# A hybrid encoder trunk in split fp32 on one core: the borders between its stages rebuilt

## The chip, the core and the metric

The kernel runs on one core of a Trainium2 chip. TensorE (PE) multiplies; its clock has two levels, 2.4 GHz and 1.2 GHz, and a profile gives the level as a share of the full one. VectorE (DVE), ScalarE (ACT) and GpSimd (POOL) do the element work, and SyncE (SP) issues nearly all DMAs, in one order. Each engine takes its instructions strictly in the order in which they stand in its own queue. The metric is the device time of one launch in microseconds, the median of three runs.

## The reference

Two layers (DEPTH = 2) over 640 tokens: 512 of one prompt, and 8 sequences of 16. A layer has three stages; each takes the residual `x`, norms and modulates it, and adds its own normed, gated output:

```
for l in range(DEPTH):
    h = rmsnorm(x, norm_g[l,0]) * (1 + sc1) + sh1
    x = x + 0.5 * g1 * rmsnorm(swiglu(h, w_ffn1[l,0], w_ffn3[l,0], w_ffn2[l,0]), norm_g[l,1])
    h = rmsnorm(x, norm_g[l,2]) * (1 + sc2) + sh2
    y, states = token_mixer(h, ...)      # 1024 -> 5640 columns, attention, mLSTM, w_pa, w_pb, w_out
    x = x + g2 * rmsnorm(y, norm_g[l,3])
    h = rmsnorm(x, norm_g[l,4]) * (1 + sc3) + sh3
    x = x + 0.5 * g3 * rmsnorm(swiglu(h, w_ffn1[l,1], w_ffn3[l,1], w_ffn2[l,1]), norm_g[l,5])
```

D_MODEL is 1024, D_FF 2816. `sh`, `sc`, `g` come from `silu(c) @ w_ada + b_ada`, one row for the prompt and one for each of the 8 sequences. All of it is fp32.

## The kernel before

**Numbers.** Each large fp32 product is three products of fp32r parts: an operand is split into `hi` (ACT copies it to fp32r) and `lo = x - hi` (DVE, sometimes POOL subtracts), and `three` issues hi·hi, hi·lo, lo·hi. So every weight slab and every activation costs an ACT cast and a subtraction before PE may use it.

**Tiles.** The 640 tokens are five tiles of 128 rows (tile 4 is the 8 sequences), and in the transposed layout, where a tile of `h` holds 128 channels by 640 tokens, two halves of 320 tokens, t=0 and t=1. Tiles 0 and 1 and half of tile 2 make t=0; the rest of tile 2 and tiles 3 and 4 make t=1.

**A stage's end.** `down` (FFN) and `out_projection` (mixer) compute rows of the output: 128 tokens by two halves of 512 columns in PSUM. `down` goes by groups: tiles 0-2 columns 0-511, tiles 0-2 columns 512-1023, then tiles 3 and 4 with all columns, with slabs of weights streamed again for each group. `out_projection` does the first 512 columns of all five tiles together, keeps the split weights of the other 512 columns, and then goes tile by tile. For each tile `first_half` and `post_norm` follow: squares on ACT, the gate on DVE, a power on POOL (line 436), residual into an `X` tile (line 577), squares again, another power, then `pre_norm`: the tile is scaled by 1/rms (lines 510 and 512), transposed on PE (line 516, 8 transposes a tile) and modulated into `x`, eight transposed fp32 tiles (lines 530 to 539). `split_half` (lines 478, 479) splits `x` into `h`.

**A stage's start.** An FFN starts with `plain_columns`: four blocks of 128 columns (two each of `w_ffn1`, `w_ffn3`), with 4 x 24 matmuls of 320 columns for t=0 and 96 for t=1; the weights come from `early_chunks` (lines 340, 341). All other columns go by `blocks`, a Strassen-Winograd scheme of 7 products for 2 x 2 blocks, which also needs sums and differences of `x` (t1 to t4), made and split by `combine` (lines 493 to 499 with 478, 479). A mixer starts with `columns(..., early=True)`: four blocks of 128 columns of `w_in`, again 96 matmuls for t=0 and 96 for t=1.

**The order.** The program is written in the order of the stages, but a scheduler sets each engine's order. Buffers are rings, which can hold work back: `X` 3 (512 KB), `raw` 4, `W` 4, `C` 8, `S` 42, `Fa` 3, and PSUM `acc` 4 and `bank` 4. A `post_norm` takes two `X` tiles, one for the residual and one as scratch `jk`. PE's background work, the `ada` products of the next modulation, is fed in by a generator, `background`.

Of the kernel before, what the change touches and what calls it, by code (L numbers as in the profile page):

```python
# [15 lines left out]
P = 128  # L16
# [3 lines left out]
SB = 8  # L20
# [22 lines left out]
def kernel(  # L43
# [417 lines left out]
    def new_forms():  # L461
# [25 lines left out]
    def combine(h, x):  # L487

        a, b = halves_of_tokens
        for k in range(HK):  # L490
            x1, x2 = x[k], x[HK + k]
            t1, t2 = F("a")[:, :TA], F("a")[:, :TA]
            DVE.tensor_tensor(t1, x1[:, b], x1[:, a], ALU.subtract)
            split_to(h["t1", k], t1)
            DVE.tensor_tensor(t2, x2[:, b], t1, ALU.subtract)  # L495
            split_to(h["t2", k], t2)
            POOL.tensor_tensor(x1[:, b], x2[:, b], x1[:, b], ALU.subtract)
            split_to(h["t3", k], x1[:, b])
            POOL.tensor_tensor(x2[:, a], x2[:, a], t2, ALU.subtract)
            split_to(h["t4", k], x2[:, a], POOL)  # L500
# [5 lines left out]
    def rms_t(xt, xn, r):  # L506

        for f in range(2):
            if f:
                ACT.activation(xn[f], xt[f], AF.Copy, scale=r)  # L510
            else:
                DVE.tensor_scalar(xn[f], xt[f], r, None, ALU.mult)
        for f in range(2):
            tr = bank()
            for q in range(4):
                PE.transpose(tr[:, P * q:P * q + P], xn[f][:, P * q:P * q + P], ident)  # L516
# [4 lines left out]
    def pre_norm(xt, xn, r, i, x, mod):  # L521
        sc, sh = mod
        at = slice(P * i, P * i + P)
        for f, tr in rms_t(xt, xn, r):
            ks = slice(4 * f, 4 * f + 4)
            if i < 4:
                for q in range(4):
                    k = 4 * f + q
                    if q:
                        ready[i] = ACT.activation(x[k][:, at], tr[:, P * q:P * q + P], AF.Identity, scale=sc[:, k, 0:1], bias=sh[:, k, 0:1]).ins  # L530
                    else:
                        DVE.tensor_scalar(x[k][:, at], tr[:, P * q:P * q + P], sc[:, k, 0:1], sh[:, k, 0:1], ALU.mult, ALU.add)
            else:
                h32 = F("a")
                v4, t4 = (y.rearrange("p (q b t) -> p q b t", q=4, b=SB) for y in (h32, tr))
                a, b = (y[:, ks, 1:9].unsqueeze(3).to_broadcast([P, 4, SB, ST]) for y in mod)
                DVE.tensor_tensor(v4, t4, a, ALU.mult)
                for q in range(4):
                    (POOL if q % 2 else DVE).tensor_tensor(b16(x[4 * f + q][:, at]), v4[:, q], b[:, q], ALU.add)
# [21 lines left out]
    def post_norm(ph, i, yg, ms, y1, gi, x, mod):  # L561

        xt, jk = X([P, DM]), X([P, DM])
        load(xt, x_src(ph, i))
        s1 = small([P, 1])
        sq, y1g = jk[:, 512:1024], jk[:, :512]
# [22 lines left out]
        pre_norm(*([y[:, :512], y[:, 512:]] for y in (xt, jk)), power(t, 1), i, x, mod)  # L589
# [4 lines left out]
    def down(ph, w, gt, g, mod, nxt):  # L594
# [3 lines left out]
        x = None if last else new_x()  # L598
# [1059 lines left out]
```

## Time and profile before

| | |
|---|---|
| median of 3 runs | 3172.83 us (3172.7 to 3174.0) |
| the profiled execution | 3172.75 us |
| its span, first to last instruction | 3171.1 us |
| PE, PEld, DVE, ACT, POOL busy | 95%, 85%, 62%, 43%, 32% |
| granted PE clock, mean | 0.981 |
| HBM over the span | 128 GB/s |

PE is busy in nearly all slices; where its row on the page drops, a stage ends and another starts: slices 0, 7, 14, 20, 26 and 33 to 34. Matmuls overlap, so a busy PE need not be at full pace; the distance of one start to the next tells the pace. `L91` is the line of a helper through which all products go, so tile names tell which stage it is: `acc<-S,S` of 128x320 are the early columns at a stage's start, `bank<-S,X` and `bank<-C,W` of 128x320 the products of the blocks, 128x512 with `W` the rows at a stage's end. `x` behind a group is the number of records.

### The profile page before, as it was taken

What the parts mean: (1) busy time and instruction counts of PE and PEld (TensorE: products, weight loads), DVE (VectorE), ACT (ScalarE), POOL (GpSimd) and SP (SyncE); (2) the same over time, 40 slices, a digit from 0 to 9 for tenths busy, and PEclk for the clock granted to TensorE, in tenths of its full rate; (3) what the DMA queues carried; (4) which work ended last, traced back from release to release, by engine and by line L of the source; (5) the groups of instructions that cost most, each with busy time, mean ns of one, the idle gap of its engine ahead of it and who ended that gap; (6) DMA issues with size and microseconds to landing.
All of it is one profiled execution on the core that took longest, in us unless ns stands there. A gap on an engine that the chain in (4) does not pass through costs nothing.

```text
span 3171.1 us, 51106 instructions
## 1 busy us (share of the span) xinstructions
PE 3024.3 (95%) x19101; PEld 2702.2 (85%) x19101; DVE 1966.8 (62%) x3665; ACT 1358.8 (43%) x2849; POOL 1024.2 (32%) x991
## 2 busy tenths in 40 slices
PE   5999999899999969999999999999999999699998
PEld 4788877899899959998859888878998998699987
DVE  5666657344675576775676665563456645678755
ACT  5333346244324353444653333562343334444444
POOL 2655403110121055661155552031001110667502
PEclk8999999899999989999999999999999999899999
DMA  7555547222324333333573555471233243233335
GB/s 218 162 169 175 162 128 226 76 91 84 121 76 119 112 110 100 107 107 127 186 236 101 158 170 160 140 231 57 81 100 101 81 125 120 67 87 87 94 125 188
DMA packets 305977, 409.08 MB, mean 129 GB/s; under 512 B 22299, under 2 KB 209031, under 8 KB 305730
## 3 DMA queue, kind: packets, MB, share of 16 engines
q1 hardware_dynamic: 301042, 394.39, 40.4%
q0 software_dynamic: 4688, 11.43, 1.1%
q8 instruction: 151, 2.47, 0.3%
q14 instruction: 96, 0.79, 0.1%
HBM read 378.60 MB, written 27.14 MB: 128 GB/s over the span
## 4 chain that ended last, share of the span: by engine, by line
PE 57%; DVE 3%; DMA 2%; ACT 1%; issue 1%; POOL 1%; SPq 0%; DVEq 0%; POOLq 0%; ACTq 0%
PE acc L91 35%; PE bank L91 18%; PE acc L80 2%; DMA S<-in_w_ffn_dram 1%; DVE S L479 0%; DMA Fv<-in_w_ada_dram 0%; DMA x<-X 0%; DVE W L300 0%; PE bank L516 0%; DVE C L479 0%; DVE Fa L495 0%; DVE W L479 0%; ACT S L530 0%; ACT S L478 0%; DMA S<-in_lam_dram 0%
## 5 line engine op out<-in xcount | busy, mean ns | idle before, releaser
L91 PE MATMUL acc<-S,W 128*128 128x320 f32 x5600 | 899.6, 312 | 4.7 <-DVE S L1579 3.1
L91 PEld LDWEIGHTS acc<-S,W 128*128 128x128 f32 x5600 | 831.5, 188 | 57.0 <-ACT W L478 23.5
L300 DVE TENSOR_TENSOR W<-raw,W 128x1024 fp32r<-128x1024 f32 (+1 forms) x228 | 283.3, 1243 | 269.8 <-ACT W L299 266.1
L91 PE MATMUL acc<-W,C 128*128 128x512 f32 x1848 | 437.2, 396 | 2.7 <-DVE W L300 2.6
L91 PEld LDWEIGHTS acc<-W,C 128*128 128x128 f32 x1848 | 344.9, 188 | 91.2 <-DVE W L300 7.5
L299 ACT CAST W<-raw 128x1024 fp32r<-128x1024 f32 (+1 forms) x228 | 239.1, 1049 | 323.2 <-PE acc L91 232.1
L91 PE MATMUL bank<-S,X 128*128 128x320 f32 x1936 | 323.0, 315 | 36.7 <-ACT X L478 20.1
L91 PEld LDWEIGHTS bank<-S,X 128*128 128x128 f32 x1936 | 296.6, 192 | 53.0 <-ACT X L478 22.3
L479 DVE TENSOR_TENSOR W<-raw,W 128x512 fp32r<-128x512 f32 (+1 forms) x244 | 223.2, 915 | 160.5 <-ACT W L478 152.9
L813 POOL TENSOR_TENSOR S<-S,K 128x320 f32<-128x320 f32 x160 | 173.8, 1102 | 283.5 <-DVE K L812 239.6
L91 PE MATMUL acc<-S,S 128*128 128x320 f32 (+1 forms) x1128 | 205.0, 338 | 26.9 <-POOL S L341 10.1
L478 ACT CAST W<-raw 128x512 fp32r<-128x512 f32 (+1 forms) x244 | 150.7, 618 | 173.9 <-PE bank L91 96.3
L91 PEld LDWEIGHTS acc<-S,S 128*128 128x128 f32 x1128 | 185.6, 203 | 40.2 <-POOL S L341 14.6
L436 POOL TENSOR_TENSOR sm<-sm,mhalf 128x1 f32<-128x1 f32 (+2 forms) x80 | 63.0, 788 | 440.6 <-DVE sm L570 199.2
L91 PE MATMUL bank<-W,C 128*128 128x512 f32 x792 | 185.0, 395 | 0.0
L479 POOL TENSOR_TENSOR C<-S,C 128x256 fp32r<-128x256 f32 x44 | 51.3, 1168 | 413.5 <-ACT C L478 413.3
L479 DVE TENSOR_TENSOR X<-raw,X 128x512 fp32r<-128x512 f32 x160 | 167.2, 1046 | 27.3 <-ACT X L478 26.3
L91 PEld LDWEIGHTS bank<-W,C 128*128 128x128 f32 x792 | 148.7, 188 | 35.6
L478 ACT CAST C<-S 128x384 fp32r<-128x384 f32 (+2 forms) x280 | 130.5, 475 | 92.4 <-PE acc L91 46.7
L478 ACT CAST X<-raw 128x512 fp32r<-128x512 f32 (+1 forms) x164 | 100.7, 616 | 141.3 <-PE bank L91 88.8
L91 PE MATMUL bank<-C,W 128*128 128x320 f32 x960 | 156.0, 310 | 3.7 <-DVE W L479 2.2
L91 PE MATMUL acc<-C,X 128*128 128x320 f32 x960 | 159.1, 311 | 0.0
(377 smaller groups left out, 4919.7 us busy)
## 6 DMA issues: line engine op xcount, KB each, us to landing
raw<-in_w_ffn_dram SPq DMA_DIRECT2D x336, 512.0 KB, 3.7
Fv<-in_w_ada_dram SPq DMA_DIRECT2D x261, 256.0 KB, 3.3
raw<-in_w_in_dram SPq DMA_DIRECT2D x64, 512.0 KB, 3.9
x<-X SPq DMA_DIRECT2D x25, 512.0 KB, 3.8
X<-x SPq DMA_DIRECT2D x25, 512.0 KB, 4.3
raw<-in_w_in_dram SPq DMA_DIRECT2D x32, 256.0 KB, 4.1
X<-in_cache_k_dram SPq DMA_DIRECT2D x16, 512.0 KB, 4.5
Fp<-in_cache_v_dram SPq DMA_DIRECT2D x32, 256.0 KB, 3.0
```

Of the source, the lines that this page charges most:

```text
L80: i = PE.matmul(out, lhsT, rhs, start=start and first is None, stop=stop and last is not None).ins
L91: i = PE.matmul(out, lhsT, rhs, start=start, stop=stop).ins
L299: ACT.copy(hi, src)
L300: DVE.tensor_tensor(lo, src, hi.bitcast(F32), ALU.subtract)
L436: pows.append(POOL.tensor_tensor(r, t, mhalf.to_broadcast([P, n]), ALU.pow).ins)
L478: i = ACT.copy(hi, src).ins
L479: (eng or DVE).tensor_tensor(lo, src, hi.bitcast(F32), ALU.subtract)
L813: POOL.tensor_tensor(gm, gm, z, ALU.mult)
```

## The change

- `out_projection` and `down` become one function, `rows_out`. The out projection now goes by the groups of `down`: 16 slabs of 512 KB in place of 8. In its last group every second slab's subtraction is POOL's.
- The next stage's four early weights are begun inside the last group's loop (`begin`), loaded by one DMA each into a `raw` tile; for an FFN after the mixer the first two lie in `C`.
- `rms_t` no longer scales the tile. It scales the identity (128x128, on DVE), and a fp32 matmul of the tile with it takes the place of each transpose.
- `post_norm` takes one `X` tile in place of two.
- At the border to a mixer there is no `x`: `pre_norm` writes `hi` from PSUM on ACT and `lo` on DVE (every fourth on POOL), tile by tile.
- `combine` works in place, splits two halves at once, and is called in the first `blocks` after its second product.
- The constants of the mixer (`late_constants`) go from the program's start into `background`.

```
     def rms_t(xt, r, d):
+        DVE.tensor_scalar(d, ident, r, None, ALU.mult)
         for f in range(2):
             tr = bank()
             for q in range(4):
-                PE.transpose(tr[:, P * q:P * q + P], xn[f][:, P * q:P * q + P], ident)
+                mm(tr[:, P * q:P * q + P], xt[f][:, P * q:P * q + P], d)
     def post_norm(ph, i, yg, ms, y1, gi, x, h, mod):
-        xt, jk = X([P, DM]), X([P, DM])
+        xt, y1g, sq = X([P, DM]), F("v"), F("a")
...
     def combine(h, x):
         for k in range(HK):
             x1, x2 = x[k], x[HK + k]
+            DVE.tensor_tensor(x1[:, a], x1[:, b], x1[:, a], ALU.subtract)
             POOL.tensor_tensor(x1[:, b], x2[:, b], x1[:, b], ALU.subtract)
+            DVE.tensor_tensor(x2[:, b], x2[:, b], x1[:, a], ALU.subtract)
+            POOL.tensor_tensor(x2[:, a], x2[:, a], x2[:, b], ALU.subtract)
+            split_to(h["t42", k], x2)
+        for k in range(HK):
+            split_to(h["t13", k], x[k])
...
+    def begin(key, slots=O):
+        out = first_weights[key] = []
+        if key[0] == "mixer":
+            wl = w_in[key[1]]
+            cols = [wl[:, off + P * e:off + P * e + P] for off in (OFF_AQ, OFF_AK) for e in range(2)]
+        else:
+            cols = [w[key][:, P * e:P * e + P] for e in range(2) for w in (w_ffn1, w_ffn3)]
+        for j, c in enumerate(cols):
+            out.append(early_chunks(c, slots if j < 2 else O))
+            yield
...
+    def rows_out(ph, w, kn, rows, g, mod, nxt, slots):
...
+        early = iter(()) if last else begin(nxt, slots)
         for grp, fs in (((0, 1, 2), (0,)), ((0, 1, 2), (1,)), ((3, 4), (0, 1))):
...
+                    whl = split(t, (2 // nf, 512 * nf), eng=POOL if nf == 2 and kn == KD and k1 else DVE)
...
+                if nf == 2:
+                    while len(first_weights.get(nxt, range(4))) < 4 * (ks[-1] + 1) // (kn - 2):
+                        if next(early, 0) == 0:
+                            break
...
+                    post_norm(ph, i, *ygs[i], y[i, 1], gi, x, h, mod)
+            if forms and fs == (1,):
+                split_half(h, x, 0)
             if not last and fs == (1,):
-                split_half(h, x, 0)
-        if not last:
-            finish_h(h, x, nxt)
+                next(early)
+        if forms:
+            split_half(h, x, 1)
+            combinations.append((h, x))
...
         put(0, 0, u, product(a12, b21), False)
+        while combinations:
+            combine(*combinations.pop())
...
-        combine(h, xT)
-        with tc.issue_after(pows[-1]):
-            late_constants()
+        combinations.append((h, xT))
```

What the scheduler makes of it at three places. First, DVE at the border from layer 0's mixer to its second FFN, right behind tile 4's transposes. Before (`Fa` from `bank` is the modulation of tile 4, lines 493 and 495 are differences of `combine`, 479 the subtractions of `lo`):

```order
L537 TENSOR_TENSOR Fa_11782<-bank_11777,scT_3660 128x512
L537 TENSOR_TENSOR Fa_11793<-bank_11788,scT_3660 128x512
L539 TENSOR_TENSOR S_11404<-Fa_11782,shT_3661 128x128
L539 TENSOR_TENSOR S_11406<-Fa_11782,shT_3661 128x128
L539 TENSOR_TENSOR S_11408<-Fa_11793,shT_3661 128x128
L539 TENSOR_TENSOR S_11410<-Fa_11793,shT_3661 128x128
L493 TENSOR_TENSOR Fa_11863<-S_11404 128x320
L495 TENSOR_TENSOR Fa_11864<-S_11408,Fa_11863 128x320
L493 TENSOR_TENSOR Fa_11877<-S_11405 128x320
L479 TENSOR_TENSOR C_11433<-Fa_11864,C_11432 128x320
L495 TENSOR_TENSOR Fa_11878<-S_11409,Fa_11877 128x320
L479 TENSOR_TENSOR C_11435<-Fa_11878,C_11434 128x320
```

Now (lines 542 and 547 modulate tile 4, 508 is a difference of `combine`, 495 the subtraction of `lo`; S_11226 to S_11232 are `lo` of t=1):

```order
L542 TENSOR_TENSOR Fa_11873<-bank_11868,scT_3631 128x512
L547 TENSOR_TENSOR S_11209<-Fa_11873,shT_3632 128x128
L547 TENSOR_TENSOR S_11211<-Fa_11873,shT_3632 128x128
L542 TENSOR_TENSOR Fa_11884<-bank_11879,scT_3631 128x512
L508 TENSOR_TENSOR S_11209<-S_11209 128x320
L508 TENSOR_TENSOR S_11210<-S_11210 128x320
L508 TENSOR_TENSOR S_11211<-S_11211 128x320
L508 TENSOR_TENSOR S_11212<-S_11212 128x320
L495 TENSOR_TENSOR S_11226<-S_11209,S_11225 128x320
L547 TENSOR_TENSOR S_11213<-Fa_11884,shT_3632 128x128
L547 TENSOR_TENSOR S_11215<-Fa_11884,shT_3632 128x128
L495 TENSOR_TENSOR S_11226<-S_11210,S_11225 128x320
```

Before, differences and their splits stand ahead of the split of t=1; now four differences of `combine` still stand ahead of it, and the rest of `combine` comes later.

Second, ACT at the same border: the early weights (line 340). Before, around tile 3's modulation (530) and tile 4's squares (581):

```order
L340 CAST S_11801<-S_11799 128x512
L530 ACTIVATE S_11405<-bank_11710,shT_3661,scT_3660 128x128
L530 ACTIVATE S_11406<-bank_11710,shT_3661,scT_3660 128x128
L530 ACTIVATE S_11407<-bank_11710,shT_3661,scT_3660 128x128
L530 ACTIVATE S_11409<-bank_11719,shT_3661,scT_3660 128x128
L530 ACTIVATE S_11410<-bank_11719,shT_3661,scT_3660 128x128
L530 ACTIVATE S_11411<-bank_11719,shT_3661,scT_3660 128x128
L340 CAST S_11807<-S_11805 128x512
L581 ACTIVATE X_11754,sm_11763<-X_11753 128x512 x2
L340 CAST S_11813<-S_11811 128x512
```

Now, at the start of the last group (299 casts the slabs of `w_out`, 585 and 599 are tile 0's squares):

```order
L340 CAST C_11606<-raw_11604 128x512
L340 CAST C_11610<-raw_11604 128x512
L299 CAST W_11416<-raw_11414 128x1024
L299 CAST W_11422<-raw_11420 128x1024
L299 CAST W_11620<-raw_11618 128x1024
L585 ACTIVATE Fa_11464,sm_11466<-bank_11363 128x512
L299 CAST W_11626<-raw_11624 128x1024
L340 CAST C_11692<-raw_11690 128x512
L340 CAST C_11696<-raw_11690 128x512
L599 ACTIVATE Fa_11464,sm_11473<-X_11462 128x512
L299 CAST W_11656<-raw_11654 128x1024
```

Two of the four early weights are now cast before tile 0's second square; the other two stand behind tile 3's modulation.

Third, PE at the border from layer 0's second FFN to layer 1's first, where the t=1 columns begin (`acc<-S,S`). Before, the third block product (`bank<-S,X`) stands right ahead of them:

```order
L91 MATMUL bank_16956<-S_15049,X_16953 128x320
L91 MATMUL bank_16956<-S_15051,X_16953 128x320
L91 MATMUL bank_16956<-S_15052,X_16953 128x320
L91 MATMUL bank_16956<-S_15051,X_16953 128x320
L91 MATMUL acc_16722<-S_15041,S_16498 128x320
L91 MATMUL acc_16722<-S_15042,S_16498 128x320
L91 MATMUL acc_16722<-S_15041,S_16499 128x320
```

Now it is the first block product:

```order
L91 MATMUL bank_16835<-S_15056,X_16832 128x320
L91 MATMUL bank_16835<-S_15058,X_16832 128x320
L91 MATMUL bank_16835<-S_15059,X_16832 128x320
L91 MATMUL bank_16835<-S_15058,X_16832 128x320
L91 MATMUL acc_16677<-S_15060,S_15953 128x320
L91 MATMUL acc_16677<-S_15061,S_15953 128x320
L91 MATMUL acc_16677<-S_15060,S_15954 128x320
```

So the 96 matmuls of t=1 moved ahead of two block products, one of them a product of `combine`'s output.

## Rows read from the trace of the kernel before

**Rows 1.** The page, busy time of the engines over the whole span.

```profile
PE 3024.3 (95%) x19101; PEld 2702.2 (85%) x19101; DVE 1966.8 (62%) x3665; ACT 1358.8 (43%) x2849; POOL 1024.2 (32%) x991
```

**Rows 2.** Windows: stretch, length; busy (x) of PE, PEld, DVE, ACT, POOL; clock.

```profile
55.96:94.89 38.93, 27.50 (x151) 26.71 (x152) 32.13 (x69) 19.21 (x48) 27.50 (x32) 0.82 0.22 67
557.26:604.34 47.08, 35.80 (x209) 34.73 (x209) 20.55 (x37) 16.66 (x41) 13.56 (x20) 0.82 0.31 94
1131.44:1205.80 74.36, 46.56 (x255) 40.15 (x255) 51.42 (x68) 35.02 (x81) 48.89 (x43) 0.84 0.32 99
1614.18:1679.54 65.36, 58.19 (x303) 40.14 (x303) 41.91 (x64) 25.88 (x62) 37.01 (x34) 0.97 0.61 199
2120.66:2165.78 45.12, 34.43 (x209) 33.37 (x210) 19.53 (x37) 16.61 (x41) 13.71 (x20) 0.85 0.31 95
2692.60:2766.78 74.18, 46.21 (x248) 42.16 (x248) 52.15 (x69) 34.50 (x79) 49.02 (x43) 0.82 0.24 71
```

**Rows 3.** Timeline of PE, mixer to FFN: start, length, instruction [idle before, releaser].

```profile
1139.98 1.97 PE L516 MATMUL bank<-ident,X 128*128 128x128 f32 x8 [8.54 <-DVE X L512]
...
1160.19 5.25 PE L91 MATMUL acc<-S,S 128*128 128x320 f32 x34 [0.76 <-POOL S L341]
1171.67 0.90 PE L91 MATMUL bank<-S,X 128*128 128x320 f32 x2 [6.22 <-ACT X L478]
1176.86 3.04 PE L91 MATMUL bank<-S,X 128*128 128x320 f32 x10 [4.29 <-DVE X L479]
...
1191.71 14.25 PE L91 MATMUL acc<-S,S 128*128 128x320 f32 x96
```

**Rows 4.** Timeline of ACT and SP, the same border.

```profile
1140.09 0.60 ACT L567 ACTIVATE X<-acc 128x512 f32<-128x512 f32 x1 [0.52 <-DMA x<-X]
...
1136.03 0.38 SPq L114 DMA_DIRECT2D x<-X  x1
```

**Rows 5.** Timeline of DVE and POOL, the same border.

```profile
1168.58 1.14 DVE L479 TENSOR_TENSOR C<-S,C 128x320 fp32r<-128x320 f32 x1
1169.65 0.48 DVE L479 TENSOR_TENSOR S<-S,S 128x320 fp32r<-128x320 f32 x1
...
1168.34 1.04 POOL L499 TENSOR_TENSOR S<-S,Fa 128x320 f32<-128x320 f32 x1 [0.83 <-DVE Fa L495]
```

**Rows 6.** Timeline of PE, first FFN to mixer in layer 0.

```profile
560.08 10.50 PE L91 MATMUL acc<-S,S 128*128 128x320 f32 x61 [2.83 <-DVE Fv L558]
570.42 1.04 PE L516 MATMUL bank<-ident,X 128*128 128x128 f32 x8
...
576.32 1.79 PE L516 MATMUL bank<-ident,X 128*128 128x128 f32 x8 [3.27 <-DVE X L512]
582.17 0.90 PE L91 MATMUL acc<-S,S 128*128 128x320 f32 x2 [4.06 <-ACT S L340]
```

**Rows 7.** Timeline of PE, second FFN of layer 0 to first of layer 1.

```profile
1660.38 1.06 PE L91 MATMUL bank<-Fv,cT 128*32 128x512 f32 x8
...
1665.47 14.23 PE L91 MATMUL acc<-S,S 128*128 128x320 f32 x96
```

**Rows 8.** Timeline of PE, the program's start.

```profile
59.03 0.70 PE L91 MATMUL acc<-S,W 128*128 128x320 f32 x3 [3.07 <-DVE S L1579]
...
83.99 0.90 PE L91 MATMUL bank<-S,X 128*128 128x320 f32 x2 [6.48 <-DVE cvec L243]
```

**Rows 9.** Groups by line: xcount | busy us, mean ns | idle.

```profile
L91 PE MATMUL bank<-S,Fa 128*128 128x128 f32 x352 | 48.5, 275 | 0.0
L516 PE MATMUL bank<-ident,X 128*128 128x128 f32 x224 | 34.9, 305 | 37.0 <-DVE X L512 23.4 <-DVE S L1533 13.6
```

**Rows 10.** Groups by line: slab splits and early weights.

```profile
L300 DVE TENSOR_TENSOR W<-raw,W 128x1024 fp32r<-128x1024 f32 x224 | 278.3, 1243 | 253.6 <-ACT W L299 249.9 <-DMA Fp<-gate 2.1
...
L341 POOL TENSOR_TENSOR S<-S,S 128x512 fp32r<-128x512 f32 x40 | 56.2, 1410 | 57.3 <-ACT S L340 56.9
...
L299 ACT CAST W<-raw 128x1024 fp32r<-128x1024 f32 x224 | 234.8, 1048 | 286.0 <-PE acc L91 195.0 <-PE bank L91 81.7 <-issue 5.5
```

More of the change, by code (lines that the diff above doesn't have):

```diff
@@ L536, in pre_norm @@
                 a, b = (y[:, ks, 1:9].unsqueeze(3).to_broadcast([P, 4, SB, ST]) for y in mod)
                 DVE.tensor_tensor(v4, t4, a, ALU.mult)
-                for q in range(4):
-                    (POOL if q % 2 else DVE).tensor_tensor(b16(x[4 * f + q][:, at]), v4[:, q], b[:, q], ALU.add)
+            for q in range(4):
+                k = 4 * f + q
+                y = x[k][:, at] if x else v[:, q]
+                if i == 4:
+                    (POOL if q % 2 and x else DVE).tensor_tensor(b16(y), v4[:, q], b[:, q], ALU.add)
+                elif q and x:
+                    ACT.activation(y, tr[:, P * q:P * q + P], AF.Identity, scale=sc[:, k, 0:1], bias=sh[:, k, 0:1])
+                else:
+                    DVE.tensor_scalar(y, tr[:, P * q:P * q + P], sc[:, k, 0:1], sh[:, k, 0:1], ALU.mult, ALU.add)
+                if not x:
+                    hh, hl = (z[:, at] for z in h[k])
+                    if i == 4:
+                        ACT.copy(hh, y)
+                    else:
+                        ACT.activation(hh, tr[:, P * q:P * q + P], AF.Identity, scale=sc[:, k, 0:1], bias=sh[:, k, 0:1])
+                    (POOL if q == 3 else DVE).tensor_tensor(hl, y, hh.bitcast(F32), ALU.subtract)
@@ L604, in down @@
             step = 4 // nf
-            for k0 in range(0, KF, step):
-                ks = range(k0, min(k0 + step, KF))
+            for k0 in range(0, kn, step):
+                ks = range(k0, min(k0 + step, kn))
                 ws, gs = {}, {}
@@ new lines, in rows_out, with down, rows @@
+                next(early)
+        if forms:
+            split_half(h, x, 1)
+            combinations.append((h, x))
+        return h
+    def down(ph, w, gt, g, mod, nxt):
+        def rows(k, o, n):
+            if n == 2 * P:
+                both = C()
+                hl = both[:, :n], both[:, n:2 * n]
+            else:
+                hl = [C()[:, :n] for _ in range(2)]
+            split_to(hl, gt[k][:, o:o + n], POOL if n == 2 * P and k % 2 else DVE)
+            return hl
+        return rows_out(ph, w, KF, rows, g, mod, nxt, O)
@@ L883, in finish @@
                 part_b.clear()
-            ready = {off + P * e: early_chunks(wl[:, off + P * e:off + P * e + P])
-                     for off, put, m0 in parts for e in range(2)} if early else {}
+            ready = iter(first_weights["mixer", l] if early else ())
             for off, put, m0 in parts:
@@ L890, in columns @@
                 for e in range(2):
-                    w = ready[off + P * e] if early else chunks(r, e)
+                    w = next(ready) if early else chunks(r, e)
                     a = acc()
```

145 lines of the change are left out of this document (41 added, 104 removed).

## The prediction, made before the changed kernel ran

> **What bounds the kernel now.** I read the page first: PE is busy for 95% of the span, the next engine for 62% [rows 1], so time can only go where PE is idle, slow or short of work. The picture of 40 slices shows PE falling at the program's start and where one stage hands over to the next; the timeline of PE gives the exact ends, and windows laid on them give lengths and counts [rows 2]. In each window I count what PE had to do at full pace. A 320-column matmul takes 14.25 / 96 = 0.148 us [rows 3], a transpose of 128 columns 0.11 us (eight in 1.04 us [rows 6], of which the last shows its whole length, 0.27; 34.9 us busy for 224, or 0.156, is the upper end [rows 9]); eight records of the `ada` products take 1.06 us [rows 7]. What is left of the window is lost, to idle time or to a low clock (0.82 to 0.85 of full in five of the six windows [rows 2]):
>
> - FFN to mixer (twice): 47.1 us with 192 matmuls and 16 transposes, 30.2 us of work, 16.9 lost; in layer 1 45.1, so 14.9 lost.
> - Mixer to FFN (twice): 74.4 us with 192 + 36 matmuls, 16 transposes, 10 `ada` records: 28.4 + 5.3 + 1.8 + 1.3 = 36.8, 37.6 lost; in layer 1 four more block matmuls and no `ada`, 38 lost.
> - Second FFN to first FFN (once): 65.4 us with 192 + 36 matmuls, 16 transposes and 58 `ada` records (7.7): 43.2, 22.2 lost.
> - The start, from 56 to 95 us: 142 matmuls and 9 small transposes, 22 of 38.9 us, 16.9 lost.
>
> Together 146.6 us. What holds PE differs. At mixer to FFN tile 4 waits for an `X` buffer: ACT starts its square at 1140.09 on a DMA [rows 4], nearly 9 us after PE had finished its rows (the window's start), because its second `X` tile had to wait for tile 3's store, issued at 1136.03 [rows 4]. Then the early weights arrive late (PE waits for POOL's line 341), then the first block products wait on casts and subtractions while ACT and DVE do `combine`, and only then do the 96 matmuls of t=1 run [rows 3]. At FFN to mixer it is 2.83 us until a PSUM buffer is free, then tile 4's chain, then an early weight [rows 6]. At FFN to FFN the 96 of t=1 stand behind three block products [rows 7]. At the start DVE carries `combine` and the constants [rows 8].
>
> **The change part by part.**
>
> *Fp32 matmul for transpose.* One matmul [128 x 128] on fp32 leaves two records: the program issues 176 matmuls of the form `bank<-S,Fa`, and the group counts 352. They take 48.5 us together, 0.276 each, against 0.156 for a transpose [rows 9]: 0.12 us more, 8 in a tile, 5 tiles, so 4.8 us more PE work at each of 5 borders, 24 us in all. The same at the start (4.8 us) lies under idle time of PE and costs nothing. Where PE idles anyway, part of the 24 costs nothing either: 12 to 24, I take 22, because tiles 0 to 2 sit among rows that keep PE busy. The shorter chain (no scaling of 512 columns on DVE and ACT, 128 on DVE instead) gives back about what the longer transposes take. The Trainium skill ("TensorE: Matmul & The Clock Gate", Terms) says that transpose mode is four times as fast for fp32; by that, as an estimate, the edit would cost 3 x 0.11 x 8 = 2.6 us a tile, 66 us for 25 tiles, and the sum would come to 3158 (rival 4). The rows say a factor of about two, against the page.
>
> *FFN to mixer.* No `x`, no `split_half`, weights cast during the last group, one `X` tile. Left is the wait for PSUM (2.8 us [rows 6], unchanged: all four `acc` hold the last rows), then 96 matmuls and tile 3's transposes cover 14.2 + 1.8 us of the chain. The last rows end at 557.26 [rows 2]; tile 3's transposes start 13.2 us later, tile 4's 19.1, with the wait for an `X` buffer in it [rows 6]. Without that wait tile 4 follows tile 3 by some 3 us, so PE comes to it last, at 2.8 + 14.2 + 1.8 = 18.8 us, and then waits only for tile 4's first modulated block, 1 to 2 us. Clock about 1. Lost 5 (2.5 to 9) where it was 16.9 and 14.9: gain 21.8 before the matmuls' price.
>
> *Mixer to FFN.* The rows by groups cost the same 240 matmuls. The slabs double: 8 more casts (1.05) and splits. In groups one and two one slab feeds 18 matmuls of 0.23, 4.2 us, against 1.05 on ACT and 1.24 on DVE: hidden. In the last group a slab feeds 12, 2.8 us; every second subtraction goes to POOL, where 1024 columns cost between 1.24 (DVE's price) and twice 1.41, 2.8 [rows 10]; I take 2.7, nearest the row of the same engine. With four subtractions of early weights (1.41 each) that is 10.8 + 5.6 = 16.4 us of POOL, and six powers, in a group of 22.3. So it fits, but a slab or a power late by one instruction shows: 4 us lost (0 to 10). The group also loads up to 17 half-megabytes in 22.3 us less four prefetched, about 300 GB/s, more than any window of rows 2 moves; that is in the 10. After the last row: tile 2's and 3's transposes, the second two weights (cast behind tile 3's modulation, as the order shows), all found room in the 96 matmuls of t=0 except some 3 us. Then DVE does four differences of `combine` ahead of the first `lo` of t=1, and POOL, with six to eight instructions of 1 to 1.7 us, the ones of every fourth: 5 us until t=1 runs freely. `combine`'s rest and the first blocks' splits then run beside t=1: DVE about 20 subtractions. One of 320 columns is 0.48 us alone and 1.14 beside POOL [rows 5], so 28 us against PE's 14 + 7 is possible, 13 against 21 too: 5 us (0 to 15). Lost 17 (8 to 30) of 37.8 each: gain 41.6.
>
> *FFN to FFN.* The last group is long (61 us), so tiles 0 to 2 are done. Left: PSUM 2.5 [rows 6], t=1's first splits 5, `combine` in the blocks 4.5: 12 (5 to 20) of 22.2, gain 10.2.
>
> *The start.* `combine` and constants leave DVE, which was busy 32.1 of 38.9 us there [rows 2]. The idle 3.07 us stay, the 6.48 behind the constants go [rows 8], some clock too; `combine` comes back in the first blocks. Gain 7 (0 to 12). The constants in `background` cost PE some twenty tiny transposes beside other work: nothing, or 2 us if not covered.
>
> Sum, against the profiled execution's 3172.75 us (span 3171.1, 1.65 outside; the median of the runs is 0.08 above): 21.8 + 41.6 + 10.2 + 7 - 22 = 58.6 us, so **3114 us**, 1.8% faster.
>
> **Rivals.**
>
> 1. *Nearly everything closes.* Each border keeps its lower end: 2 x 2.5 + 2 x 8 + 5 lost, start 12 gained, 24 for the matmuls: 31.8 - 5 + 75.6 - 16 + 22.2 - 5 + 12 - 24 = 91.6, 3081 us. For it: the named waits are each removed by a buffer or by order. Against: DVE and POOL together are busy 100.3 us in the 74.4 us of mixer to FFN [rows 2], and that work stays.
>
> 2. *The read port decides.* DVE's subtractions of two SBUF operands and POOL's work run at each other's cost [rows 5]. If they simply queue, mixer to FFN keeps 30 each, FFN to FFN 20, the start nothing: 21.8 + 15.6 + 2.2 + 0 - 22 = 17.6, 3155 us. The Trainium skill ("SBUF — State Buffer", Who interferes with whom) says so: with both operands in SBUF, DVE and a POOL instruction that reads SBUF exclude each other for a whole instruction. By that rule moving subtractions to POOL saves nothing, and it is this rival's time; rows 5 agree for that pair, 1.14 against 0.48, but the casts on ACT and PE's work go on.
>
> 3. *Slower.* The waits only change their place: as rows come by groups, tiles 3 and 4 finish together rather than one after the other, and what t=0 covers is lost again in the last group, where DVE, POOL and DMA must bring slabs and weights too. Then the borders lose what they lost, and the matmuls' 22 to 24 us come on top: 3196 us. It decides once the borders give back less than 22 us together. For it: the order puts four differences ahead of t=1. Against: the 9 us wait for `X` and the late weights cannot come back in that form.
>
> 4. *The matmul is dearer than two records.* If it holds PE for four transposes' time, 0.11 x 4, each of the 25 x 8 costs 0.33 more, 66 us: 58.6 + 22 - 66 = 14.6, 3158 us. The count of records and their busy time speak against it [rows 9].
>
> **How the numbers follow.** The forecast gets 0.57, with its own range 3095 to 3140; the first rival 0.2, the second 0.14, the third 0.06, the fourth 0.03. A range of 8 in 10 reaches from 3080, which cuts half of the first rival, to 3156, past most of the second. The forecast and first rival are faster; of the second and fourth I count nine tenths. A change within 0.2%, 6 us, can't be told from none; it would be the thin end of rivals 2 and 4. Faster 0.92, same 0.03, slower 0.05.
>
> **What would show it.** In the changed profile: (a) 480 records of 128x128 on the transposes' line and a mean spacing near 0.11; (b) no wait of ACT for `x<-X` at tile 4's square; (c) PE's waits for line 341 gone at FFN to mixer and few at mixer to FFN; (d) lost time, counted as above, of 5, 17 and 12 us; (e) POOL nearly full in the out projection's last group; (f) idle PE ahead of `acc<-S,C` or `bank<-C,W`, whose operands come from `combine`; (g) the clock at 0.95 or more in these windows. Wrong it is if PE stalls for slabs (`W` from line 300) in the out projection's last group by more than 10 us, or if lost time appears in the blocks instead.

## The result and the profile after

The changed kernel takes 3125.85 us (median of 4 runs, 3123.87 to 3127.47) against 3172.76 in the same session: a ratio of 0.9852, 95% interval [0.9835, 0.9869], 46.9 us less. The forecast was 3114 in a range of 3080 to 3156: the direction and the range hold, the gain is 12 us short of the 58.6 forecast. The profiled execution has a span of 3122.1 us and a mean clock of 0.992.

The page, busy time of the engines, to be read beside [rows 1]:

```profile
PE 3027.2 (97%) x19341; PEld 2712.0 (87%) x19341; DVE 2005.5 (64%) x3745; ACT 1345.4 (43%) x2799; POOL 1039.4 (33%) x987
```

PE's busy time has hardly changed (3 us more), with 240 records more; what went is time in which PE was idle or slow. The same borders as in [rows 2], from the end of the last rows (the start: from a wait of PE) to the end of t=1; the third row is a stretch inside the rows, behind a wait of PE:

```profile
53.50:87.30 33.80, 27.86 (x179) 25.98 (x172) 28.79 (x53) 16.82 (x39) 19.68 (x15) 0.95 0.23 64
558.44:594.00 35.56, 32.83 (x226) 32.00 (x226) 17.58 (x53) 11.98 (x35) 6.50 (x14) 1.00 0.27 86
525.12:530.20 5.08, 5.08 (x15) 4.04 (x16) 3.29 (x9) 2.17 (x4) 2.32 (x3) 0.66 0.96 305
1126.61:1175.05 48.44, 37.90 (x244) 36.35 (x243) 42.36 (x59) 25.87 (x62) 33.84 (x31) 0.89 0.36 112
1593.51:1633.54 40.03, 37.77 (x247) 35.38 (x246) 33.09 (x48) 17.30 (x42) 24.58 (x24) 0.96 0.41 132
2097.83:2133.29 35.46, 32.76 (x226) 31.92 (x226) 17.59 (x53) 11.94 (x35) 6.58 (x14) 1.00 0.27 87
2664.64:2712.08 47.44, 36.94 (x243) 35.38 (x242) 41.42 (x58) 25.96 (x62) 33.66 (x31) 0.89 0.29 87
```

Where the gain lies can be worked out from the two traces: PE issues the same 14,496 products of 320 and 512 columns in both (without the `ada` products), so the lead of the changed kernel, how much earlier it is, can be read at the start of the n-th of them. The lead grows in steps; the forecast's terms stand beside them, less 4.4 us a border for the matmuls:

| place | forecast, us | measured, us |
|---|---|---|
| start and first FFN | 7 | 5.5 |
| FFN to mixer, layers 0 and 1 | 13.0 | 4.8 + 3.7 |
| mixer to FFN, layers 0 and 1 | 32.8 | 14.6 + 17.0 |
| second FFN to first | 5.8 | 3.9 |
| last rows of the program | 0 | -1.8 |
| elsewhere | 0 | 0.1 |
| sum | 58.6 | 47.8 |

Behind the last product another 1.2 us are gained: the spans differ by 49.0. The first step varies by itself: profiles of runs that leave the start as it is in the changed kernel differ from it there by -1.5 to +1.0 us.

PE at mixer to FFN in layer 0, beside [rows 3]:

```profile
1124.65 2.12 PE L91 MATMUL acc<-W,S 128*128 128x512 f32 x8 [1.25 <-POOL W L300]
1126.61 1.95 PE L91 MATMUL bank<-Fa,X 128*128 128x128 f32 x16
1129.84 0.56 PE L91 MATMUL acc<-S,C 128*128 128x320 f32 x2 [1.29 <-ACT S L494]
...
1156.88 0.90 PE L91 MATMUL bank<-S,X 128*128 128x320 f32 x2 [7.57 <-ACT X L494]
1158.63 8.93 PE L91 MATMUL acc<-S,C 128*128 128x320 f32 x44 [0.85 <-ACT S L722]
...
1169.76 5.45 PE L91 MATMUL acc<-S,S 128*128 128x320 f32 x36
```

Of the four waits of [rows 3], 19.8 us together, one long one is left, 7.57 us ahead of t=1, and the 44 products behind it run at 0.20 us each; the 36 at the end take 0.15. The long wait ends with ACT's cast of a weight (`X`) for a block's product that stands ahead of t=1 in PE's order. ACT makes it behind t=1's casts, and for the last of those it had waited for DVE:

```profile
1154.62 1.18 ACT L494 CAST S<-S 128x320 fp32r<-128x320 f32 x3 [4.30 <-DVE S L547]
...
1156.22 0.61 ACT L494 CAST X<-raw 128x512 fp32r<-128x512 f32 x1
```

```profile
1148.21 3.63 DVE L508 TENSOR_TENSOR S<-S 128x320 f32<-128x320 f32 x4
1151.77 1.55 DVE L495 TENSOR_TENSOR S<-S,S 128x320 fp32r<-128x320 f32 x1
1153.24 1.55 DVE L547 TENSOR_TENSOR S<-Fa,shT 128x128 f32<-128x128 f32 x2
1154.71 5.87 DVE L495 TENSOR_TENSOR S<-S,S 128x320 fp32r<-128x320 f32 x5
```

The four differences of `combine` (line 508) stand ahead of the rest of tile 4's modulation (line 547) and of t=1's subtractions (line 495), and those take 1.2 to 1.55 us each, against 0.48 alone [rows 5]. At FFN to mixer the waits of [rows 6] have shrunk to 0.65 us for PSUM and 1.04, 0.61 and 0.44 around tile 4, but a new one stands earlier, in the last group's rows (3.34 us in layer 1):

```profile
525.12 7.18 PE L91 MATMUL acc<-W,C 128*128 128x512 f32 x23 [3.39 <-DVE W L300]
```

```profile
521.83 0.63 ACT L599 ACTIVATE Fa<-X 128x512 f32<-128x512 f32 x1 [1.06 <-DVE X L595]
522.36 0.19 ACT L599 ACTIVATION_READ_ACCUMULATOR Fa<-X 128x1 f32 x1
522.45 1.03 ACT L299 CAST W<-raw 128x1024 fp32r<-128x1024 f32 x1
```

The slab's cast on ACT stands behind tile 2's square, and that waits for DVE: two residual adds (line 595) took 2.90 us there, beside POOL's subtractions, and 1.41 at 1128.77. In the stretch after the wait the clock is 0.66 (third window above).

### The profile page after: what moved, and what is told of

Same layout as the page of the kernel before. It is cut to its first block, busy times and chain, and to the rows that moved or that the text cites. A ratio compares the mean times of both kernels' runs of the same rounds, so it can differ in the third digit from the quotient of the medians.

```text
span 3122.1 us, 51546 instructions
## 1 busy us (share of the span) xinstructions
PE 3027.2 (97%) x19341; PEld 2712.0 (87%) x19341; DVE 2005.5 (64%) x3745; ACT 1345.4 (43%) x2799; POOL 1039.4 (33%) x987
## 4 chain that ended last, share of the span: by engine, by line
PE 88%; DVE 5%; DMA 3%; ACT 2%; issue 1%; POOL 1%; SPq 0%; DVEq 0%; POOLq 0%; ACTq 0%
PE acc L91 52%; PE bank L91 30%; PE acc L80 4%; DMA raw<-in_w_ffn_dram 1%; DVE W L300 1%; DMA raw<-in_w_in_dram 1%; ACT W L299 1%; PE bank L1098 0%; DVE S L508 0%; DVE S L495 0%; POOL W L300 0%; DMA S<-in_w_ada_dram 0%; DMA Fv<-in_w_ada_dram 0%; PE bank L1215 0%; PE bank L1056 0%
## 5 line engine op out<-in xcount | busy, mean ns | idle before, releaser
L91 PE MATMUL acc<-S,W 128*128 128x320 f32 x4640 | 748.2, 313 | 7.1 <-ACT S L1563 3.1
L91 PEld LDWEIGHTS acc<-S,W 128*128 128x128 f32 x4640 | 688.1, 188 | 61.4 <-issue 23.9
L300 DVE TENSOR_TENSOR W<-raw,W 128x1024 fp32r<-128x1024 f32 x240 | 305.0, 1271 | 282.3 <-ACT W L299 280.9
L91 PE MATMUL acc<-W,C 128*128 128x512 f32 x1848 | 440.9, 398 | 10.9 <-DVE W L300 10.9
L299 ACT CAST W<-raw 128x1024 fp32r<-128x1024 f32 x248 | 260.0, 1049 | 364.7 <-PE acc L91 270.2
L91 PE MATMUL bank<-S,X 128*128 128x320 f32 x1936 | 314.9, 310 | 15.1 <-ACT X L494 15.1
L495 DVE TENSOR_TENSOR W<-raw,W 128x512 fp32r<-128x512 f32 (+1 forms) x244 | 216.8, 889 | 155.8 <-ACT W L494 151.1
L91 PEld LDWEIGHTS bank<-S,X 128*128 128x128 f32 x1936 | 290.7, 188 | 25.7 <-ACT X L494 16.5
L91 PE MATMUL acc<-C,W 128*128 128x320 f32 x1728 | 273.7, 310 | 0.0
L91 PEld LDWEIGHTS acc<-C,W 128*128 128x128 f32 x1728 | 258.1, 188 | 5.1 <-issue 5.0
L495 DVE TENSOR_TENSOR X<-raw,X 128x512 fp32r<-128x512 f32 x160 | 163.3, 1021 | 28.3 <-ACT X L494 26.9
L91 PE MATMUL acc<-S,X 128*128 128x320 f32 x976 | 166.6, 311 | 0.0
L91 PEld LDWEIGHTS acc<-S,X 128*128 128x128 f32 x976 | 148.1, 188 | 19.3 <-issue 12.6
```

What stands on the lines that cost most here:

```text
L91: i = PE.matmul(out, lhsT, rhs, start=start, stop=stop).ins
L300: (eng or DVE).tensor_tensor(lo, src, hi.bitcast(F32), ALU.subtract)
L495: (eng or DVE).tensor_tensor(lo, src, hi.bitcast(F32), ALU.subtract)
```

## The experiments

Each was timed against the kernel before on the same chip; before had medians of 3170.2 to 3172.6 us there.

**Transposes put back** (in the changed kernel)

```
-        DVE.tensor_scalar(d, ident, r, None, ALU.mult)
+        ACT.activation(xn[1], xt[1], AF.Copy, scale=r); DVE.tensor_scalar(xn[0], xt[0], r, None, ALU.mult)
-                mm(tr[:, P * q:P * q + P], xt[f][:, P * q:P * q + P], d)
+                PE.transpose(tr[:, P * q:P * q + P], xn[f][:, P * q:P * q + P], ident)
```

> The changed kernel with the transposes put back (scaled halves in two F tiles, 8 transposes a tile), everything else as changed. Theory, the prediction's term: a tile's sixteen fp32 records take 1.95 us in the changed kernel's trace and its eight transposes 1.04 before, so 0.91 us a tile; four tiles at each of five borders stand in a busy PE, 20 x 0.91 = 18 us, and tile 4's may be hidden: 3104 to 3112 us. Rival: the shorter chain is worth what the records cost (scaling 512 columns on DVE and ACT puts 0.6 to 1.3 us into tile 4's chain at each border, and into the others' buffers): 3120 to 3130 us.

The program's start has transposes again too. 3119.63 us, 0.9838 [0.9824, 0.9851]: 6 us below the changed kernel by the medians, 4 by the ratios, and the intervals overlap. The rival, mostly. The lead over the changed kernel grows by 3.6 us at the start, and by 0.9 with each tile among the rows (2.7 a border); behind the rows it is lost again: the steps over whole borders are -1.0 and -3.4 (FFN to mixer), 3.1 and 1.2 (mixer to FFN), -0.7.

**Two X tiles again** (in the changed kernel)

```
-        xt, y1g, sq = X([P, DM]), F("v"), F("a")
+        xt, jk = X([P, DM]), X([P, DM]); sq, y1g = jk[:, 512:1024], jk[:, :512]
```

> The changed kernel with the second X tile in post_norm put back as scratch. Theory, the prediction's: the X ring made tile 4 wait, some 8 us at each border from mixer to FFN and 2 to 3 at the others, so 20 to 25 us come back: 3146 to 3151 us, with ACT waiting at tile 4's square for the load. Rival: with tiles 3 and 4 in one group, and their loads asked for long before, the ring no longer matters: under 3 us, 3126 to 3129.

3147.36 us, 0.9923 [0.9909, 0.9936]: the theory's size, 21.5 us slower, but not its places. All of it is at mixer to FFN (14.3 and 12.2 us); the other three borders change by under 1 us, and the last rows get 1.8 back.

**First early weight later**

```
-            if not last and fs == (1,):
+            if not last and fs == (1,) and kn == KD:
                 next(early)
...
```

> The changed kernel, but down asks for its first early weight inside the last group and no longer at the end of the second: on SP its DMA moves behind six slabs, the other engines keep their order. Theory A: the wait of 3.4 us for a slab in down's last group comes from the raw buffer that the early weight holds (the slab's DMA is issued the moment POOL's line 341 has ended), so it goes: 2 to 3.4 us at three borders, 3116 to 3121 us. Rival B: the slab's cast stands behind tile 2's square on ACT, which waits for DVE; the wait stays and the time too, 3124 to 3128.

3126.13 us, 0.9859 [0.9846, 0.9873]; the wait is 3.39 us as before. Time and wait are as rival B has them, but B is not settled by it: the `raw` buffers of the early weights are freed as late as before, so theory A was hardly touched.

**All early weights in the second half of down's last group**

```
-  while len(first_weights...) < 4 * (ks[-1] + 1) // (kn - 2):
+  while len(first_weights...) < (4 * (ks[-1] + 1) // (kn - 2) if kn == KD else (ks[-1] - 9) // 3):
...
```

> The changed kernel, but down begins its four early weights only in the second half of the last group. Theory: the early weights' share of raw buffers, ACT and POOL while tile 2 is normed makes PE's wait of 3.4 us for a slab; it goes at both borders from FFN to mixer: 3118 to 3121 us. Rival 1: tile 2's own chain on ACT and DVE makes it, the wait stays: 3124 to 3128. Rival 2: the weights come late and PE waits for them after the rows, as in the kernel before: 3127 to 3136.

3127.72 us, 0.9864 [0.9849, 0.9879]: the wait goes, as in the theory, but the time is that of the rivals. The 3.39 us are gone, so the early weights' work made that wait; PE then waits in the rest of the group instead, 3.55 us in six waits:

```profile
521.18 4.93 PE L91 MATMUL acc<-W,C 128*128 128x512 f32 x20 [0.50 <-DVE W L300]
...
535.26 7.73 PE L91 MATMUL acc<-W,C 128*128 128x512 f32 x32 [0.51 <-DVE W L300]
543.90 1.20 PE L91 MATMUL acc<-W,C 128*128 128x512 f32 x4 [0.91 <-ACT W L299]
545.39 7.72 PE L91 MATMUL acc<-W,C 128*128 128x512 f32 x32 [0.29 <-DVE W L300]
553.40 1.20 PE L91 MATMUL acc<-W,C 128*128 128x512 f32 x4 [0.29 <-ACT W L299]
555.65 2.13 PE L91 MATMUL acc<-W,C 128*128 128x512 f32 x8 [1.05 <-DVE W L300]
```

Moving that work to the second half of the group is worth nothing. Which of ACT, DVE, POOL and the `raw` ring binds there was not tried apart.

**`combine` behind t=1's subtractions**

```
             while combinations:
-                combine(*combinations.pop())
+                with <each instruction ordered after the last line-495 subtraction of t=1 on its engine>:
+                    combine(*combinations.pop())
...
```

> The changed kernel with the differences and splits of combine ordered behind t=1's last subtractions on DVE and POOL. Theory, the prediction's step: four differences (3.6 us on DVE) stand ahead of t=1's splits, and without them t=1 starts 3 to 4 us earlier at each border from mixer to FFN and 1 to 3 at FFN to FFN, while blocks hide the rest: 3115 to 3119 us. Rival: PE waits there for ACT (casts of a block's operand and the Silu that frees PSUM stand behind t=1's casts), or what is gained at t=1 comes back in the first blocks: 3123 to 3130.

3116.29 us, 0.9829 [0.9815, 0.9842]: the theory, 9.6 us by the medians and 7.3 by the ratios. The intervals of the two ratios still touch, but no run of one kernel lies among those of the other. The trace shows 3.5 and 2.7 us at mixer to FFN, nothing at second to first FFN, where the theory had 1 to 3, and 8.5 in all. PE and DVE at the same place now:

```profile
1152.14 5.62 PE L91 MATMUL acc<-S,C 128*128 128x320 f32 x26 [4.59 <-ACT S L725]
1158.88 2.92 PE L91 MATMUL acc<-S,C 128*128 128x320 f32 x18 [1.13 <-DVE S L495]
```

```profile
1154.04 3.73 DVE L510 TENSOR_TENSOR S<-S 128x320 f32<-128x320 f32 x4
1157.68 1.14 DVE L495 TENSOR_TENSOR S<-S,S 128x320 fp32r<-128x320 f32 x1
```

The edit orders `combine` behind the last subtraction in the order of the program, and the scheduler put another one behind it: one of t=1's six on DVE still stands behind the four differences, in both layers, and PE waits 1.13 us for it. So the run shows a part of what they cost. The block's product that stood ahead of t=1 on PE is no longer there either.

**The same, and t=1's first two products in other PSUM buffers**

```
-                b.append(ubs.pop(0) if first else acc())
+                b.append(ubs.pop(0) if first else (acc if e else bank)())
```

> The differences of combine held behind t=1's splits, and besides the first two products of t=1 of an FFN accumulate in bank buffers instead of acc. Theory: with the differences gone from the way, t=1's start waits 4.6 us for the Silu that frees an acc buffer and stands behind t=1's casts on ACT; with banks it waits for the splits alone: 3 to 4 us less at each border from mixer to FFN, 3107 to 3112 us. Rival: the splits on DVE (1.2 to 1.5 us each beside POOL) are as late as the Silu, and PE only changes what it waits for: 3114 to 3118 us.

3118.94 us, 0.9834 [0.9821, 0.9848]: the rival. PE starts t=1 4.0 us after tile 4's records begin, where it was 8.7, and then waits for DVE's subtractions (seven waits in the program, 12.3 us in all, longest 4.7). The two borders change by 0.3 and -1.7 us; the rest of what separates the two traces lies at the start, which the edit leaves alone.

**Matmuls only for tiles 3 and 4**

```
-  pre_norm(..., power(t, 1), sq[:, :P], i, x, h, mod)
+  pre_norm(..., power(t, 1), [y1g, sq] if i < 3 else sq[:, :P], i, x, h, mod)   # a list: scale and transpose
...
```

> The changed kernel with transposes (and the scaled tile) at the program's start and for tiles 0 to 2 of each border, fp32 matmuls for tiles 3 and 4 alone. Theory after the run with transposes everywhere: PE pays 0.91 us a tile wherever it is busy, and tile 4's chain pays 2 to 3 us a border for the scaling, so the two balanced there; here only the first is undone: 3 x 0.91 x 5 = 13.7 us and some 3 at the start, 3109 to 3115 us. Rival: scaling 512 columns on DVE and ACT for tiles 0 to 2 slows the slabs of the last group by as much: 3119 to 3126 us.

3116.61 us, 0.9827 [0.9814, 0.984]: between the two, nearer the theory: 9.2 us, of which the start gives 3.3 and the borders 1.4, 2.5, 0.2, 0.5 and 1.2. The 2.7 us that each border's rows save are mostly lost again to waits behind them. Against the run with transposes everywhere, matmuls for tiles 3 and 4 alone gain 6.6 us over the five borders (2.4, -0.6, 0.9, 3.9 and 0.0): that much the shorter chain of these two tiles is worth beyond its records.

**One X tile in the kernel before**

```
-        xt, jk = X([P, DM]), X([P, DM]); sq, y1g = jk[:, 512:1024], jk[:, :512]
+        xt, y1g, sq = X([P, DM]), F("v"), F("a")     # scaled halves go to y1g and sq
```

> The kernel before with one X tile in post_norm (the scaled halves go to the dead scratch tiles), nothing else changed. Theory, the prediction's: the X ring's wait is 8.5 and 7.6 us of idle PE at the two borders from mixer to FFN and 3 us at the others, so 15 to 22 us go: 3150 to 3157 us. Rival: the late early weights (line 341), 5 us behind it, and combine in front of t=1 take most of its place: 3162 to 3170 us.

3163.11 us, 0.9972 [0.9962, 0.9983], 9 us less: the rival. In the kernel before, the 8.54 us of [rows 3] stand ahead of tile 3's transposes (1139.98), not of tile 4's, which come at 1149.33, among the products of t=0. Tile 3's square waited for a buffer as well:

```profile
1127.66 2.80 PE L91 MATMUL acc<-W,S 128*128 128x512 f32 x11
...
1149.33 0.60 PE L516 MATMUL bank<-ident,X 128*128 128x128 f32 x4
```

```profile
1131.84 0.60 ACT L567 ACTIVATE X<-acc 128x512 f32<-128x512 f32 x1 [1.11 <-DMA x<-X]
```

With one `X` tile, tile 3's transposes come 1.4 us after the last rows (1126.37), where it was 9.5 (1139.98 less 1130.46), and tile 4's 11.0, where it was 18.9 (1149.33 less 1130.46), so the ring did hold both for 8 us. But PE now idles as long ahead of tile 4, 8.46 us, as it did ahead of tile 3:

```profile
1123.44 2.93 PE L91 MATMUL acc<-W,S 128*128 128x512 f32 x12
...
1127.81 0.63 PE L516 MATMUL bank<-ident,Fv 128*128 128x128 f32 x4 [0.55 <-ACT Fa L510]
1128.27 0.60 PE L516 MATMUL bank<-ident,Fa 128*128 128x128 f32 x4
1137.33 1.09 PE L516 MATMUL bank<-ident,Fv 128*128 128x128 f32 x4 [8.46 <-DVE Fv L512]
...
1138.92 1.41 PE L91 MATMUL acc<-S,S 128*128 128x320 f32 x4
```

```profile
1137.10 0.62 ACT L340 CAST S<-S 128x512 fp32r<-128x512 f32 x1 [0.27 <-DMA S<-in_w_ffn_dram]
```

Tile 4's own chain takes that time: ACT makes its first square at 1126.41 and its next ones at 1133.15 and 1134.47, behind tile 3's modulation and t=0's casts. The other work that PE could do, t=0, stands behind tile 4 in PE's order, and its first weight is cast at 1137.10, when its DMA has landed. t=0 starts 12.6 us after the rows; in the kernel before, 11.8.

**Matmuls for transposes in the kernel before**

```
-                PE.transpose(tr[:, P * q:P * q + P], xn[f][:, P * q:P * q + P], ident)
+                mm(tr[:, P * q:P * q + P], xt[f][:, P * q:P * q + P], d)     # d = ident * r
```

> The kernel before with fp32 matmuls by a scaled identity for the transposes, nothing else changed. Theory, the prediction's term: PE pays 0.91 us a tile, and only where it idles is a part free: 17 to 23 us slower, 3189 to 3195 us. Rival after the run with transposes in the changed kernel: tile 4's chain at each border is 2 to 3 us shorter and gives most of it back: 3172 to 3180 us.

3219.49 us, 1.0146 [1.0132, 1.016]: 46.9 us slower, outside both. The matmul reads the residual's `X` tile itself, not a scaled copy, and the scaled identity lies in the second one, so both are free only when PE has done the matmuls; with two of three `X` buffers in use by each tile, the tiles come one after the other. PE idles before tiles 2 and 3, and the sixteen records behind each wait take twice as long as 1.95, at a clock of 0.50 and 0.52. SP issues the next `X` load as the sixteen records before it end (1138.96 and 1149.08):

```profile
1145.32 3.76 PE L91 MATMUL bank<-X,X 128*128 128x128 f32 x16 [6.37 <-issue]
1157.37 3.72 PE L91 MATMUL bank<-X,X 128*128 128x128 f32 x16 [8.29 <-issue]
```

```profile
1139.03 0.32 SPq L114 DMA_DIRECT2D X<-x  x1
...
1149.16 0.32 SPq L114 DMA_DIRECT2D X<-x  x1
```

**Both gains together, and POOL's sums held too**

```
+        with <ordered after t=1's last line-495 subtraction on POOL>:      # the second kernel only
             POOL.tensor_tensor(s1, a21, a22, ALU.add)
             POOL.tensor_tensor(s2, s1, a11, ALU.subtract)
```

> Both edits that gained, together: transposes at the start and for tiles 0 to 2, and combine held behind t=1's splits. Theory: they act at different places (the rows of the last group; t=1), so 9.2 and 7.3 to 9.5 us add: 3107 to 3110 us. Rival: both only bring PE earlier to the same wait, t=1's subtractions on DVE, and overlap: 3113 to 3117 us.

> As the kernel with both edits, and besides POOL's two sums for the first block (lines 757 and 758, 1.3 to 1.5 us each) are held behind t=1's splits. Theory: DVE's subtractions of t=1 take 1.2 to 1.5 us each while POOL reads SBUF and 0.48 alone, so with POOL quiet t=1's splits are done 3 to 4 us earlier: 2 to 3 us less at each border from mixer to FFN than with both edits alone, and the subtractions in the trace are below 0.8 us. Rival: the first block's products come that much later and PE waits there instead: no gain, or 2 to 4 us more.

3109.49 us, 0.9802 [0.9788, 0.9815], and 3108.68 us, 0.9798 [0.9785, 0.9811]. The first adds up as its theory says and beats both kernels: 16 us below the changed one. The second is right in part about DVE, and its rival about the time. DVE's subtractions of t=1 without the sums held, and with them held:

```profile
1140.54 1.34 DVE L495 TENSOR_TENSOR S<-S,S 128x320 fp32r<-128x320 f32 x1
...
1142.63 5.60 DVE L495 TENSOR_TENSOR S<-S,S 128x320 fp32r<-128x320 f32 x4
```

```profile
1141.58 0.47 DVE L495 TENSOR_TENSOR S<-S,S 128x320 fp32r<-128x320 f32 x1
...
1142.80 4.51 DVE L495 TENSOR_TENSOR S<-S,S 128x320 fp32r<-128x320 f32 x5
```

1.40 us each against 0.90, and one of 0.47 that began while POOL was idle. With the sums held all six stand ahead of the differences; without, the sixth is still behind them. t=1 starts after 1.9 us of waits instead of 4.1, but the first blocks then wait for their operands (1.57 us at one place), and the 0.8 us between the medians is within the intervals.

**All slab subtractions on DVE**

```
-  whl = split(t, (2 // nf, 512 * nf), eng=POOL if nf == 2 and kn == KD and k1 else DVE)
+  whl = split(t, (2 // nf, 512 * nf), eng=DVE)
```

> The changed kernel with all subtractions of slabs in the out projection's last group on DVE, none on POOL. Theory A: POOL takes four of eight off a DVE that is needed for the tiles' chains; without it 4 x 1.24 us more on DVE in each of two groups make PE wait for slabs: 3130 to 3138 us. Theory B, the prediction's second rival: DVE and POOL take turns at their read port, so the move to POOL saves nothing: 3122 to 3128 us.

3124.76 us, 0.9849 [0.9836, 0.9863]: no difference, the time of theory B. Its mechanism is not shown by that: with all on DVE, PE waits for no slab in the last group, where it waited 2.7 us, and is 4.6 and 4.8 us further on by the end of t=0, but waits longer ahead of t=1 (9.7 us instead of 7.57). Over the whole borders 1.5 and 0.5 us are left.

## Why the prediction was right, and where its sum was not

**Fp32 matmul for transpose.** The count and the pace were right: `bank<-Fa,X` has 448 records and `bank<-Fa,S` 32 (a), sixteen in 1.95 us, so 0.91 us a tile where 0.96 was forecast, and rival 4 is out.

```profile
L91 PE MATMUL bank<-Fa,X 128*128 128x128 f32 x448 | 57.7, 285 | 14.7 <-ACT S L1522 11.9 <-ACT S L557 2.1 <-DVE Fa L522 0.5
```

The Trainium skill ("TensorE: Matmul & The Clock Gate", Terms) gives transpose mode four times the speed for fp32; here the matmul is two records at a transpose's pace, a factor of two. Wrong is the step to the time. I took 22 us as the edit's net cost, its shorter chain as only balancing its longer records, and the start as free. Undone, the edit is worth 4 to 6 us: at the borders the longer chain of tiles 3 and 4 and waits behind the rows take back all that the rows save (-0.8 us over the five), while the start, which I had under idle PE, pays 3.6, of which 1 to 1.5 can be the start's own variation. With 4 to 6 in the place of 22, the rest of the sum, forecast at 80.6 us, came to 51 to 53; the errors partly cancelled. And in the kernel before, with two `X` tiles, the edit costs 46.9. No number of its own could be right for both kernels. That the two edits by themselves make this difference follows from how long each holds an `X` tile, but no run has the pair without the other changes, so it is not shown.

**The X ring.** (b) holds: no ACT wait for `x<-X` at tile 4's square. But I put the 9 us of [rows 3, 4] down to tile 4 and counted them as idle time that goes with the ring. They stood ahead of tile 3's transposes, and without the ring's hold PE idles as long ahead of tile 4, whose chain and the early weights are no earlier; one `X` tile alone gives 9 us over the whole program. In the changed kernel the second tile costs 21.5. There the weights are ready and the matmuls hold the residual's tile until PE has read it; which of the two makes the ring count was not tried apart.

**Mixer to FFN.** Lost time counted as in the prediction, in layer 0: 48.4 us with 192 products (28.4), 48 fp32 records (5.9) and two of a block (0.3) leave 13.8, and 2.7 us of waits for slabs in the last group: 16.5, forecast 17 (d). The parts were not as forecast. The last group loses 2.7 (4), and the run with all subtractions on DVE, in which these waits are gone, shows that POOL's share made them. Its POOL time is 16.3 us, as I had it (16.4), but the group is 30.3 us long with its tiles' records and waits, not 22.3, so (e), POOL nearly full, is wrong. t=0 loses 2.1 (3). Ahead of t=1 stand 8.4 us of idle PE and then 44 products in 8.8 us where 6.5 would do, 10.7 against 5. Holding the differences of `combine` back gives 3.5 and 2.7 of these; that much of the cause is proven. The sign (f) was not the right one: `acc<-S,C` are early columns here, whose weights lie in `C`, and the 7.57 us stand ahead of `bank<-S,X`. PE has no wait in the blocks, against 5; 1.0 of the 16.5 is not placed. That the sum came so near 17 is luck: two errors cancelled. That DVE's subtractions slow down beside POOL was rival 2's mechanism, and the rule of the Trainium skill ("SBUF — State Buffer", Who interferes with whom), that a DVE instruction with two SBUF inputs contends with a POOL instruction that reads SBUF, agrees with the trace, 0.47 us begun with POOL idle and 1.34 beside POOL's sum. The rival's price, 30 us a border, was far too high: 16.5 were lost.

**FFN to mixer.** After the rows 35.5 us with 28.4 + 3.9 of work: 3.2 lost, forecast 5. The step that failed is "weights cast during the last group" at no cost: that group now holds early weights and tile by tile `hi` and `lo` beside its slabs, and PE loses 3.4 us to one late slab, and, at a clock of 0.66, about 1.8 more in the fourteen products behind it (5.08 us where 3.3 would do). The prediction looked for such stalls in the out projection's last group only. The runs show that the early weights make that wait, and that their work costs as much in the second half of the group, the one other place that was tried.

**Second to first FFN.** Lost in the window: 40.0 us less 28.4, 3.9, ten `ada` records (1.3) and twelve of a block (1.9), so 4.5, forecast 12. Yet only 3.9 us of lead came. The step that failed is the price of the `ada` records, 0.13 us each from [rows 7], where eight stand together. In both kernels many come in twos, and two take the time of eight. From start to next start, less waits, the 58 took 20.2 us in the window before, not 7.7, so some 12 of the 22.2 that I counted as lost were theirs. Of them 48 now stand behind the window: among the 940 products there, the same in both kernels, 120 take 26.9 us where 78 took 16.5. The first line is of the kernel before, in that window:

```profile
1641.33 9.34 PE L91 MATMUL bank<-Fv,cT 128*32 128x512 f32 x22 [0.20 <-DMA Fv<-in_w_ada_dram]
```

```profile
1666.57 1.04 PE L91 MATMUL bank<-Fv,cT 128*32 128x512 f32 x2
```

**The last rows** lose 1.8 us, not forecast. It goes with the one `X` tile: the kernel before loses 1.8 with it, the changed kernel gets 1.8 back without it. In the traces it is a wait for a slab, 1.45 us in the changed kernel and 1.46 in the kernel before with one tile, which the two kernels with two tiles do not have; how the `X` tile makes it was not followed.

(c) holds: PE waits for line 341 nowhere (10.1 us in 12 waits before). (g), a clock of 0.95, holds at FFN to mixer (1.00) and second to first FFN (0.96), and fails at mixer to FFN (0.89), behind the wait of 7.57 us.

So the range held because each border's waits were named and bounded, and because errors in the terms fell both ways. Of the 12 us missing the traces place 10.9: 4.5 at FFN to mixer, where a cost was set to nothing, 1.9 at second to first FFN, where the `ada` records were priced too low, 1.8 at the end, 1.5 at the start and 1.2 at mixer to FFN.

## What to carry to other kernels

Edits that touch one ring of buffers cannot be priced one by one: here one was worth -9 or -21.5 us and another +47 or +5, depending on the kernel that it stood in. When a wait is to be removed, ask what the waiting engine could do instead, and when that is ready: here a held buffer, the next tile's chain and late weights ran side by side, and the profile names only the one that came last. Price a record from the place where it stands: eight `ada` records together took as long as two. Work that is moved "under" a full stretch still takes its engines' slots there, and a stall it makes costs PE more than its idle time.

## What the runs showed of the hardware

After the longer waits shown here PE ran on at a low granted clock, as a mean of its two levels over the stretch: 0.66 behind 3.4 us of idle time, and 0.72 over the 44 products behind 7.57 and 0.85 us, a third more time for those products. It was 1.00 over the 36 products at the end.

```profile
1158.63:1167.40 8.77, 8.77 (x44) 8.77 (x45) 8.77 (x10) 4.32 (x8) 6.92 (x6) 0.72 0.03 6
1169.76:1175.05 5.29, 5.29 (x39) 5.29 (x38) 5.29 (x7) 1.87 (x4) 3.56 (x3) 1.00 0.00 0
```

Scaling a 128x128 identity on DVE took 0.28 us in one tile and 1.30 in another, where POOL was subtracting from SBUF.
